# Column tiles by seven products: sums made in open PSUM banks and copied out by ScalarE, instead of added on VectorE

## The chip, the cores and the metric

The kernel runs on one core of a Trainium2 chip. A core has five engines that work side by side and wait for one another by semaphores: TensorE (PE; its weight loads are the row PEld), VectorE (DVE), ScalarE (ACT), GpSimd (POOL) and SyncE (SP), which here issues the transfers between the chip's memory and SBUF. TensorE writes its results to PSUM, which has eight banks of 128 x 512 float32; VectorE and ScalarE read them from there. The metric is the device time of one execution in microseconds (us), less being better; a run's time stands beside that of the kernel before on the same chip.

## The reference

One decoder layer over 2048 tokens (and 16 meta tokens ahead of them) of width 1024. A wide projection of the normalised input feeds two attention branches and four gates:

```python
xn = rms_norm(h, norm_gain[l])
proj = xn @ w_in[l]
sb_q, sb_k, sb_v, sw_q, sw_k, sw_v, sb_z, sw_z, g_sb, g_sw = jnp.split(proj, offsets, axis=-1)
o_sb = stick_breaking_attention(...)
...
o_sw = sliding_window_sink_attention(...)
y_sb = (o_sb * jax.nn.silu(sb_z)) @ w_branch_sb[l]
y_sw = (o_sw * jax.nn.silu(sw_z)) @ w_branch_swa[l]
merged = jax.nn.sigmoid(g_sb) * y_sb + jax.nn.sigmoid(g_sw) * y_sw
h = h + merged @ w_out[l]
```

The change touches how a part of the gates is made: `silu(sb_z)`, `silu(sw_z)`, `sigmoid(g_sb)` and `sigmoid(g_sw)`, each a block of columns of `proj` followed by its function.

## The kernel before

**Tiles and precision.** The projection is cut into column tiles of 128 columns and groups of 512 tokens (four groups, 0 to 3). The first half of the kernel treats groups 2 and 3, the second groups 0 and 1. Each factor is split into a high and a low part (`wh`, `wl` for weights, `xh`, `xl` for the input), and a product of a weight and an input takes three matmuls: high by high, high by low, low by high. A plain column tile over one group runs over 8 blocks of 128 of the width: 24 matmuls (line 1188).

**Pairs.** In a stage of each half, column tiles are made two at a time (`gate_pairs`). Two tiles c and d, two token groups `ga` and `gb` and the two halves of the width form a product of 2 x 2 blocks, which is made with seven block products instead of eight, by sums and differences of blocks. A block product is 4 blocks of the width by three matmuls, so 12 matmuls (lines 1929 to 1931). The first half has eight pairs, the second four. `t1` to `t4` are combinations of the input blocks, made once; `s1` to `s4` are combinations of the weight blocks, made for each pair by `pair_weights`: VectorE makes four sums (`r1` to `r4`), ScalarE rounds each to its high part (line 1877), VectorE subtracts to get the low part (line 1879). In the first half `pair_weights` also splits the loaded weights themselves (ScalarE line 116, VectorE line 120); in the second half the split weights come from memory. There are three buffers for `wh` and `wl` and four for the high and low parts of `s`, so those of the next pair are written as TensorE finishes with the ones in use.

**What happens behind the products, before.** Each of the seven products goes to a PSUM bank of its own, in turn over six banks (the tags g, z and t with two each). ScalarE copies the first product (line 1953), and VectorE makes seven additions of a PSUM bank and an SBUF tile (line 1935), which give the four results of a pair. A result then gets its function: ScalarE's sigmoid (lines 1940 and 1943), for the `z` gates a multiplication on VectorE (line 1941), and a store. The results, the `r` and the sigmoids all live in nine buffers of 128 x 512 named `tmp`.

**Beside the pairs.** `along` is a generator that the loop advances once per pair. In the first half it is `sums_ahead`, which loads the next half's rows and squares them on ScalarE (line 1892, four squares a step), and ends with a logarithm and an exponential (lines 133 and 134). In the second half it is `output_weight_sums`, loads, VectorE sums and stores for the last stage. `between`, at the last pair of the first half, scales the next half's input (`prep`).

**Order.** TensorE's instructions run in the order in which they are written. ScalarE's and SyncE's in these stages, and VectorE's from the middle of the first pair on, are put in order at build time by a planner, which walks through its own model of the times and takes, for an engine that is free, the earliest written instruction that can go. On the chip each engine then keeps that order strictly, whatever the times turn out to be.

Of the kernel before, what the change touches and what calls it, by code (L numbers as in the profile page):

```python
# [10 lines left out]
AF = mybir.ActivationFunctionType  # L11
# [5 lines left out]
P = 128  # L17
# [32 lines left out]
def tile_kernel(ctx, tc, x, xt, meta, metat, gain, w_in, w_sb, w_sw, w_out, sinks, fgain,  # L50
# [8 lines left out]
    def DMA(dst, src):  # L59
        return nc.sync.dma_start(*(t.bitcast(F32) if t.dtype == F32R else t for t in (dst, src)))  # L60
# [6 lines left out]
    def ps(tag):  # L67
        return pp.tile([P, 512], F32, tag=tag, name="ps_" + tag, bufs={"g": 2, "z": 2, "t": 2, "o": 2}[tag])
# [1043 lines left out]
    def tmp(dt=F32, rows=P):  # L1112
        return tp.tile([rows, GT], dt, tag="tmp", name="tmp", bufs=9)
# [112 lines left out]

    sums_back = []

    def sb_k(p):
        def use(g, acc, ms):  # L1230
            h, l = tmp(F32R), low(acc)
            evac_split(h, l, acc)
            for i, t in enumerate((h, l)):
                DMA(kd[p][g][i][:, :GT], t)
            if ms is not None:
                def later():
                    mc = meta_cols(sums_back[p] if p < 2 else ms, "t" if p < 2 else "o")
                    h, l = tmp(F32R)[:, :NM], tmp(F32R)[:, :NM]
                    A.copy(h, mc)
                    V.tensor_tensor(l, mc, f32(h), op=ALU.subtract)  # L1240
                    for i, t in enumerate((h, l)):
                        DMA(kd[p][3][i][:, GT:], t)
                pending.append(later)
        return weights(C_SBK + p * P), use, True

    def sb_q(p):
        def use(g, acc, ms):
            h, l = tmp(F32R), low(acc)
            evac_split(h, l, acc, 0.125)
            DMA(qd[p][g][0], h)  # L1250
            DMA(qd[p][g][1], l)
        return weights(C_SBQ + p * P), use, False

    def to_rows(acc, hv, lv):

# [24 lines left out]
            for queue in (soon, late, pending):  # L1280
                flush(queue)

    def sb_v(p):

        def use(g, acc, ms):
            t, d = tmp(), tmp()
            A.copy(t, acc)
            V.tensor_tensor(d[:, :GT - 1], t[:, 1:], acc[:, :GT - 1], op=ALU.subtract)
            A.copy(vf[:, p, g % 2 * 4:g % 2 * 4 + 4], t.rearrange("p (b q) -> p b q", b=4)[:, :, 0])

            def join(nxt):
                V.tensor_tensor(d[:, GT - 1:], nxt, t[:, GT - 1:], op=ALU.subtract)
                if g % 2 == 0:
                    A.copy(vn[:, p:p + 1], t[:, 0:1])

# [12 lines left out]

            def meta():
                mc = meta_cols(ms)  # L1310
                m = tmp()
                mv, md = m[:, :NM + 1], m[:, 32:32 + NM]
                G.memset(mv[:, NM:], 0.0)
                A.copy(mv[:, :NM], mc)
                V.tensor_tensor(md, mv[:, 1:], mv[:, :NM], op=ALU.subtract)
                join(mv[:, 0:1])

                def turned():
                    tr = ps("t")
                    T.transpose(tr[:NM, :P], md, ident)  # L1320
                    meta_rows(tr[:NM, :P], vm[0:NM, p, :, 0:64], vm[0:NM, p, :, 64:128])
                    for n in (NM, 2 * NM, 4 * NM):
                        DMA(vm[n:2 * n, p], vm[0:n, p])
                    rows()
                soon.append(turned)

            if ms is None:
                join(vn[:, p:p + 1] if g % 2 else vf[:, p, 4:5])
            pending.append(rows if ms is None else meta)
            if g % 2 == 0:  # L1330
                for a, t in enumerate(vfirst):
                    r = slice(64 * a, 64 * a + 64)
                    G.tensor_copy(t[r, p], vf[r, p])
        return weights(C_SBV + p * P), use, "back"

    def gate(c0, dst, silu):
        def use(g, acc, ms):
            e = tmp()
            A.activation(e, acc, AF.Sigmoid)  # L1339
            if silu:  # L1340
                V.tensor_tensor(e, acc, e, op=ALU.mult)
            DMA(dst[g], e)
        return weights(c0), use, False

    def tiles_by_tile(makes, groups, meta=False, bank="g"):
        for mk in makes:
# [570 lines left out]
    def gate_pairs(ga, gb, pairs, pool, sums_x, nxt, ordered, along, between):  # L1917

        t1, t2, t3, t4 = sums_x[:4]
        b11, b21 = ((xh[ga][:, j:j + HK, :], xl[ga][:, j:j + HK, :]) for j in (0, HK))  # L1920
        b22 = xh[gb][:, HK:, :], xl[gb][:, HK:, :]

        banks = iter(range(1 << 30))

        def product(a, b):
            acc = ps("gzt"[next(banks) % 3])
            (wh, wl), (h, l) = a, b
            for k in range(HK):
                T.matmul(acc, lhsT=wh[:, k, :], rhs=h[:, k, :], start=k == 0, stop=False)  # L1929
                T.matmul(acc, lhsT=wh[:, k, :], rhs=l[:, k, :], start=False, stop=False)  # L1930
                T.matmul(acc, lhsT=wl[:, k, :], rhs=h[:, k, :], start=False, stop=k == HK - 1)  # L1931
            return acc

        def add(t, acc, u):
            V.tensor_tensor(t, acc, u, op=ALU.add)

        def gate_out(dst, t, silu):
            if silu:
                e = tmp()
                A.activation(e, t, AF.Sigmoid)  # L1940
                V.tensor_tensor(t, t, e, op=ALU.mult)
            else:
                A.activation(t, t, AF.Sigmoid)
            DMA(dst, t)

        for n, ((_, cdst, csilu), (_, ddst, dsilu)) in enumerate(pairs):
            a11, a12, a22, s1, s2, s3, s4 = nxt
            end = n + 1 == len(pairs)
            if n and not end:
                nxt = []  # L1950
                drain(pair_weights(pairs[n + 1][0][0], pairs[n + 1][1][0], pool, nxt))
            p, u, v, w = (tmp() for _ in range(4))
            A.copy(p, product(a11, b11))
            more = product(a12, b21)
            add(u, product(s2, t2), p)
            add(p, more, p)
            if not n:
                nxt = []
                ordered()
                drain(pair_weights(pairs[1][0][0], pairs[1][1][0], pool, nxt))  # L1960
            gate_out(cdst[ga], p, csilu)
            next(along, None)
            if end:
                between()
# [5 lines left out]
            gate_out(cdst[gb], v, csilu)  # L1970
            add(u, product(s3, t3), u)
            add(w, p5, u)
            gate_out(ddst[gb], w, dsilu)
            add(u, p4, u)
            gate_out(ddst[ga], u, dsilu)


    sbt = [lambda p=p, f=f: f(p) for f, p in ((sb_k, 0), (sb_k, 1), (sb_q, 0), (sb_v, 0), (sb_v, 1), (sb_q, 1),
                                              (sb_k, 2), (sb_v, 2), (sb_q, 2), (sb_k, 3), (sb_v, 3), (sb_q, 3))]
    sbz, swz, gsb, gsw = ([(c + p * P, dst[p], dst in (zs, zw)) for p in range(len(dst))]  # L1980
                          for c, dst in ((C_SBZ, zs), (C_SWZ, zw), (C_GSB, gs), (C_GSW, gw)))
    specs = (gsb + gsw[:6] + swz + sbz + gsw[6:], sbz + gsb + gsw)

    halves = ([2, 3], [0, 1])
    g0, g1 = halves[0]
# [165 lines left out]
    held = pending[:]  # L2151
    del pending[:]
    for half, groups in enumerate(halves):
        gts = [lambda spec=spec: gate(*spec) for spec in specs[half]]
        if half == 1:
            with tc.tile_pool(name="fast1", bufs=1, side="left") as bp:
                byhand, hand = ExitStack(), ExitStack()
# [5 lines left out]
                pairs = list(zip(swz[::2], swz[1::2]))  # L2163
# [88 lines left out]
            drain(side)  # L2252
        if half == 0:
            with tc.tile_pool(name="fast", bufs=1, side="left") as bp:
                pairs = list(zip(specs[0][-FAST::2], specs[0][-FAST + 1::2]))
# [120 lines left out]
```

## Time and profile before

| | |
|---|---|
| runs, median of 3 | 2048.16 us (2047.28 to 2048.32) |
| span of the profiled execution, first to last instruction | 2045.8 us |
| TensorE busy | 2031.7 us (99%), 10375 matmuls |
| VectorE busy | 1649.3 us (81%) |
| ScalarE busy | 1177.5 us (58%) |
| the pairs' stage, first half | about 581 to 734 us |
| the pairs' stage, second half | about 778 to 854 us |

The profiled execution's time is known as its span; the runs' times include what lies around it. The profile gives, for groups of instructions, the line, engine, operation, tiles written and read and count, then busy time, the mean duration in ns, and the idle time of the engine before them with what ended it. In the order of time a row is the start, the duration, the instruction, and in brackets the idle time before it and its releaser. Busy time on TensorE overlaps: a matmul of 128 x 512 is shown with 0.39 us, but one starts every 0.23 us.

### The profile page before, as it was taken

The numbers are of one execution on the slowest core, as the hardware profiler recorded it, in microseconds if no ns is written. First come the engines' busy times: TensorE is split into PE (matmuls) and PEld (weight loads), VectorE is DVE, ScalarE is ACT, GpSimd is POOL, SyncE is SP. The second block draws the span as 40 slices with busy tenths as digits, with TensorE's granted clock in tenths as the row PEclk, the third lists the DMA queues.
The fourth block names the chain that finished last, engine by engine and source line by source line (L and its number), as shares of the span: only waits on it lengthen the run. The fifth ranks groups of instructions, "written<-read, shape, count | busy, mean of one in ns | idle before, by whom it ended". The sixth has DMA issues, their size and how long they took to land.

```text
span 2045.8 us, 31245 instructions
## 1 busy us (share of the span) xinstructions
PE 2031.7 (99%) x10375; PEld 1706.3 (83%) x10375; DVE 1649.3 (81%) x2708; ACT 1177.5 (58%) x2825; POOL 311.4 (15%) x642
## 2 busy tenths in 40 slices
PE   9999999999999999999999999999999999999998
PEld 7888888888888888888888888888888888887887
DVE  7898986877788789658887389999997788788788
ACT  6677775576755343358777366667766442335234
POOL 1233444431000000003333101000000003000000
PEclk9999999999999999999999999999999999999999
DMA  9855554865468669844344554344323779886942
GB/s 336 321 197 199 179 200 165 260 194 170 135 233 306 228 214 315 309 147 162 132 178 150 173 156 116 115 127 126 109 83 105 266 257 313 290 284 200 307 150 98
DMA packets 184065, 409.32 MB, mean 200 GB/s; under 512 B 25280, under 2 KB 29760, under 8 KB 183904
## 3 DMA queue, kind: packets, MB, share of 16 engines
q1 hardware_dynamic: 183616, 407.06, 59.0%
q8 instruction: 82, 1.34, 0.3%
q14 instruction: 79, 0.65, 0.1%
q10 hardware_dynamic: 288, 0.27, 0.0%
HBM read 256.36 MB, written 148.32 MB: 198 GB/s over the span
## 4 chain that ended last, share of the span: by engine, by line
PE 95%; ACT 2%; DVE 2%; DMA 1%; issue 1%; POOL 0%; SPq 0%; ACTq 0%; DVEq 0%; POOLq 0%
PE ps_g L1188 35%; PE ps_o L1700 6%; PE ps_z L1643 6%; PE ps_t L1668 6%; PE ps_z L1188 3%; PE ps_z L1484 3%; PE ps_o L1540 2%; PE ps_t L1518 1%; PE ps_g L1929 1%; PE ps_g L1930 1%; PE ps_g L1931 1%; PE ps_o L338 1%; PE ps_o L337 1%; PE ps_o L339 1%; PE ps_z L1929 1%; PE ps_z L1930 1%
## 5 line engine op out<-in xcount | busy, mean ns | idle before, releaser
L1188 PE MATMUL ps_g<-xh,wh 128*128 128x512 f32 x1088 | 442.3, 406 | 0.1
L1188 PE MATMUL ps_g<-xl,wh 128*128 128x512 f32 x1088 | 426.2, 392 | 0.7 <-DVE xl L2001 0.6
L1188 PE MATMUL ps_g<-xh,wl 128*128 128x512 f32 x1088 | 425.7, 391 | 0.0
L1653 DVE TENSOR_TENSOR_SCAN row<-row 128x512 f32<-128x512 f32 (+4 forms) x256 | 288.6, 1128 | 47.6 <-POOL row L1648 30.7
L1188 PEld LDWEIGHTS ps_g<-xh,wl 128*128 128x128 f32 x1088 | 204.2, 188 | 45.5 <-DVE wl L2049 0.4
L1646 ACT ACTIVATE row<-ps_z 128x512 f32<-128x512 f32 (+4 forms) x352 | 175.1, 509 | 110.3 <-PE ps_z L1643 106.3
L1188 PEld LDWEIGHTS ps_g<-xl,wh 128*128 128x128 f32 x1088 | 205.3, 189 | 34.5 <-DVE xl L2001 2.0
L1188 PEld LDWEIGHTS ps_g<-xh,wh 128*128 128x128 f32 x1088 | 204.9, 188 | 34.1 <-ACT xh L2000 0.6
L128 DVE SCALAR_TENSOR_TENSOR wtl<-ps_t,wth 128x512 fp32r<-128x512 f32 (+1 forms) x320 | 188.2, 588 | 11.3 <-ACT wth L127 11.1
L127 ACT ACTIVATE wth<-ps_t 128x512 fp32r<-128x512 f32 (+1 forms) x320 | 171.6, 536 | 41.9 <-PE ps_t L1668 39.4
L1643 PE MATMUL ps_z<-kt,q 128*128 128x512 f32 (+4 forms) x704 | 184.1, 350 | 0.7 <-ACT row L1646 0.7
L1668 PE MATMUL ps_t<-ident,row 128*128 128x128 f32 x1088 | 172.3, 273 | 1.8 <-DVE wtl L128 1.6
L1668 PEld LDWEIGHTS ps_t<-ident,row 128*128 128x128 f32 x1088 | 133.1, 140 | 35.7 <-DVE wtl L128 5.8
L1643 PEld LDWEIGHTS ps_z<-kt,q 128*128 128x128 f32 x704 | 123.8, 188 | 24.1 <-ACT row L1646 3.1
L1700 PE MATMUL ps_o<-wth,vc 128*128 128x512 f32 (+1 forms) x320 | 134.9, 422 | 0.0
L1492 ACT ACTIVATE sc<-sc,nm 128x129 f32<-128x129 f32 x256 | 100.0, 393 | 30.3 <-DVE nm L1490 29.2
L1700 PE MATMUL ps_o<-wtl,vc 128*128 128x512 f32 (+1 forms) x320 | 116.6, 364 | 0.2 <-DVE wtl L128 0.2
L1659 POOL COPY mr<-row 128x16 f32<-128x16 f32 x128 | 33.3, 263 | 382.3 <-DVE row L1653 347.7
L1477 POOL COPY sc<-skb 128x4 f32<-128x4 f32 x64 | 16.0, 256 | 458.0 <-PE ps_g L1931 304.0
L1339 ACT ACTIVATE tmp<-ps_g 128x512 f32<-128x512 f32 x63 | 37.8, 599 | 78.7 <-PE ps_g L1188 72.7
L1651 DVE TENSOR_TENSOR_SCAN row<-row,mask 128x512 f32<-128x512 f32 (+2 forms) x64 | 69.6, 1093 | 16.1 <-ACT row L1646 16.0
L1524 POOL TENSOR_SCALAR_AFFINE_SELECT pm<-ph 64x256 fp32r<-64x256 f32 x128 | 62.2, 486 | 114.7 <-ACT ph L127 110.5
(926 smaller groups left out, 4684.3 us busy)
## 6 DMA issues: line engine op xcount, KB each, us to landing
wh<-h_in_w_in SPq DMA_DIRECT2D x66, 512.0 KB, 4.0
wl<-l_in_w_in SPq DMA_DIRECT2D x66, 512.0 KB, 5.3
raw<-in_w_in SPq DMA_DIRECT2D x57, 512.0 KB, 5.6
h_in_w_in<-wh SPq DMA_DIRECT2D x50, 512.0 KB, 3.1
l_in_w_in<-wl SPq DMA_DIRECT2D x50, 512.0 KB, 4.2
q<-qd SPq DMA_DIRECT2D x128, 128.0 KB, 3.1
vc<-vd SPq DMA_DIRECT2D x48, 256.0 KB, 3.1
kd<-tmp SPq DMA_DIRECT2D x32, 256.0 KB, 3.2
```

Of the source, the lines that this page charges most:

```text
L127: A.activation(h, acc, AF.Copy, scale=scale)
L128: V.scalar_tensor_tensor(l, acc, scale, f32(h), op0=ALU.mult, op1=ALU.subtract)
L1188: T.matmul(acc, lhsT=a[:, k, :], rhs=b[:, k, :], start=k == i == 0, stop=k == KT - 1 and i == 2)
L1484: T.matmul(acc[:, a * 256:(a + 1) * 256], lhsT=lq, rhs=kk[:, 2 * kv + hl, blk * P:(blk + 2) * P], start=hl == 0, stop=hl == 1)
L1492: A.activation(sc[:, hh, :], sc[:, hh, :], AF.Exp, bias=nm[:, hh:hh + 1], accum_out=den[:, hh:hh + 1])
L1524: G.affine_select(out=pm[to, :, c], in_=full[r, :, c], pattern=[[0, 4], [sign, HB]], compare_op=ALU.is_ge, fill=0.0, base=n - 1, channel_m ...
L1643: T.matmul(z[:, :m], lhsT=qt[:, j * P:(j + 1) * P], rhs=kt[h][:, k0 + c:k0 + c + m], start=t == 0, stop=t == 1)
L1646: A.activation(r[:, c:c + m], z[:, :m], AF.Sigmoid, scale=-1.0)
L1651: V.tensor_tensor_scan(r[:, :w], r[:, :w], mask[:, :w], 1.0, op0=ALU.mult, op1=ALU.max)
L1653: V.tensor_tensor_scan(r[:, :w], r[:, :w], r[:, :w], last[j] if n else 1.0, op0=ALU.mult, op1=ALU.min)
L1668: T.transpose(tr[:, j * P:(j + 1) * P], rows_of[h, g, n - (j > i), j][:, k0:k0 + P], ident)
L1700: T.matmul(o[:, :n], lhsT=v, rhs=r, start=first and r is wh, stop=last)
```

## The change

In both stages the first pair goes on as before (`separate`). All others are made by `opened`, with three banks instead of seven. The first bank takes product 1, is copied by ScalarE, takes product 3 on top of it, is copied, takes product 5 on top, is copied, and takes product 7. The second bank takes product 2. The third takes product 4, is copied, and takes product 6 on top. So the running sums form in PSUM, and a matmul that adds to a bank has to wait for the copy out of it. VectorE adds three times per pair (one of them between two SBUF tiles), ScalarE copies four times. The products come in another order: the one with `s1` is now the fourth, `s3` the fifth, `s4` the sixth and `a22` the seventh (before: `s4`, `a22`, `s1`, `s3`). The last result's sigmoid reads the PSUM bank. The gates are put out by the same `use` function as those of plain column tiles, which for that gets the weights' loader as an argument; that part makes no instruction of its own.

```diff
-        def product(a, b):
-            acc = ps("gzt"[next(banks) % 3])
+        def product(a, b, acc=None, stop=True):
+            start = acc is None
+            if start:
+                acc = ps("gzt"[next(banks) % 3])
...
+        def copied(acc):
+            t = tmp()
+            A.copy(t, acc)
+            return t
...
+        def separate(w, cuse, duse, middle):
+            a11, a12, a22, s1, s2, s3, s4 = w
             p, u, v, w = (tmp() for _ in range(4))
             A.copy(p, product(a11, b11))
             more = product(a12, b21)
             add(u, product(s2, t2), p)
             add(p, more, p)
...
+            middle()
+            out_of(cuse, ga, p)
+            yield
             p3 = product(s4, b22)
             p4 = product(a22, t4)
             p5 = product(s1, t1)
             add(v, p5, u)
             add(v, p3, v)
...
+        def opened(w, cuse, duse):
+            a11, a12, a22, s1, s2, s3, s4 = w
+            one = product(a11, b11, stop=False)
+            p = copied(one)
+            other = product(a12, b21)
+            product(s2, t2, one, False)
+            u = copied(one)
+            add(p, other, p)
+            out_of(cuse, ga, p)
+            yield
+            two = product(s1, t1, stop=False)
+            w = copied(two)
+            product(s3, t3, one, False)
+            v = copied(one)
+            product(s4, b22, two)
+            add(w, w, v)
+            out_of(duse, gb, w)
+            add(u, two, u)
+            out_of(cuse, gb, u)
+            product(a22, t4, one)
+            duse(ga, one, None)
...
+            steps = opened(this, cuse, duse) if n else separate(this, cuse, duse, middle)
+            next(steps)
+            next(along, None)
+            if end:
+                between()
+            drain(steps)
```

More of the change, by code (lines that the diff above doesn't have):

```diff
@@ L1227, in tile_kernel, with sb_k @@
     sums_back = []
-    def sb_k(p):
+    def sb_k(p, w=weights):
         def use(g, acc, ms):
@@ L1243, in use, with sb_q @@
                 pending.append(later)
-        return weights(C_SBK + p * P), use, True
-    def sb_q(p):
+        return w(C_SBK + p * P), use, True
+    def sb_q(p, w=weights):
         def use(g, acc, ms):
@@ L1251, in use @@
             DMA(qd[p][g][1], l)
-        return weights(C_SBQ + p * P), use, False
+        return w(C_SBQ + p * P), use, False
     def to_rows(acc, hv, lv):
@@ L1281, in flush_all, with sb_v @@
                 flush(queue)
-    def sb_v(p):
+    def sb_v(p, w=weights):
         def use(g, acc, ms):
@@ L1333, in use, with gate @@
                     G.tensor_copy(t[r, p], vf[r, p])
-        return weights(C_SBV + p * P), use, "back"
-    def gate(c0, dst, silu):
+        return w(C_SBV + p * P), use, "back"
+    def gate(c0, dst, silu, w=weights):
         def use(g, acc, ms):
-            e = tmp()
+            e = acc if spare[0] and not silu else tmp()
             A.activation(e, acc, AF.Sigmoid)
@@ L1342, in use @@
             DMA(dst[g], e)
-        return weights(c0), use, False
+        return w(c0), use, False
     def tiles_by_tile(makes, groups, meta=False, bank="g"):
@@ L1923, in gate_pairs, with out_of @@
         banks = iter(range(1 << 30))
-        def product(a, b):
-            acc = ps("gzt"[next(banks) % 3])
+        def product(a, b, acc=None, stop=True):
+            start = acc is None
+            if start:
+                acc = ps("gzt"[next(banks) % 3])
             (wh, wl), (h, l) = a, b
             for k in range(HK):
-                T.matmul(acc, lhsT=wh[:, k, :], rhs=h[:, k, :], start=k == 0, stop=False)
-                T.matmul(acc, lhsT=wh[:, k, :], rhs=l[:, k, :], start=False, stop=False)
-                T.matmul(acc, lhsT=wl[:, k, :], rhs=h[:, k, :], start=False, stop=k == HK - 1)
-            return acc
+                T.matmul(acc, lhsT=wh[:, k, :], rhs=h[:, k, :], start=start and k == 0, stop=False, skip_group_check=True)
+                T.matmul(acc, lhsT=wh[:, k, :], rhs=l[:, k, :], start=False, stop=False, skip_group_check=True)
+                T.matmul(acc, lhsT=wl[:, k, :], rhs=h[:, k, :], start=False, stop=stop and k == HK - 1, skip_group_check=True)
+            return acc
+        def copied(acc):
+            t = tmp()
+            A.copy(t, acc)
+            return t
         def add(t, acc, u):
             V.tensor_tensor(t, acc, u, op=ALU.add)
[L1937 to L1951, printed above, removed]
+        def out_of(use, g, t):
+            spare[0] = True
+            use(g, t, None)
+            spare[0] = False
+        def separate(w, cuse, duse, middle):
+            a11, a12, a22, s1, s2, s3, s4 = w
             p, u, v, w = (tmp() for _ in range(4))
@@ L1956, in gate_pairs @@
             add(p, more, p)
[L1957 to L1964, printed above, removed]
+            middle()
+            out_of(cuse, ga, p)
+            yield
             p3 = product(s4, b22)
@@ L1969, in gate_pairs, with middle @@
             add(v, p3, v)
-            gate_out(cdst[gb], v, csilu)
+            out_of(cuse, gb, v)
             add(u, product(s3, t3), u)
             add(w, p5, u)
-            gate_out(ddst[gb], w, dsilu)
+            out_of(duse, gb, w)
             add(u, p4, u)
-            gate_out(ddst[ga], u, dsilu)
-    sbt = [lambda p=p, f=f: f(p) for f, p in ((sb_k, 0), (sb_k, 1), (sb_q, 0), (sb_v, 0), (sb_v, 1), (sb_q, 1),
+            out_of(duse, ga, u)
+        def opened(w, cuse, duse):
[14 more added lines that the diff above has]
+            add(w, w, v)
+            out_of(duse, gb, w)
+            add(u, two, u)
+            out_of(cuse, gb, u)
+            product(a22, t4, one)
+            duse(ga, one, None)
+        for n, ((_, cuse), (_, duse)) in enumerate(pairs):
+            end = n + 1 == len(pairs)
+            this = nxt
+            if n and not end:
+                nxt = []
+                drain(pair_weights(pairs[n + 1][0][0], pairs[n + 1][1][0], pool, nxt))
+            def middle():
+                nonlocal nxt
+                nxt = []
+                ordered()
+                drain(pair_weights(pairs[1][0][0], pairs[1][1][0], pool, nxt))
+            steps = opened(this, cuse, duse) if n else separate(this, cuse, duse, middle)
[4 more added lines that the diff above has]
+            drain(steps)
+    sbt = [lambda w=weights, p=p, f=f: f(p, w) for f, p in ((sb_k, 0), (sb_k, 1), (sb_q, 0), (sb_v, 0), (sb_v, 1), (sb_q, 1),
                                               (sb_k, 2), (sb_v, 2), (sb_q, 2), (sb_k, 3), (sb_v, 3), (sb_q, 3))]
@@ L1982, in tile_kernel, with pairs_of @@
     specs = (gsb + gsw[:6] + swz + sbz + gsw[6:], sbz + gsb + gsw)
+    def pairs_of(makes):
+        made = [mk(lambda c0: c0)[:2] for mk in makes]
+        return list(zip(made[::2], made[1::2]))
     halves = ([2, 3], [0, 1])
@@ L2153, in tile_kernel @@
     for half, groups in enumerate(halves):
-        gts = [lambda spec=spec: gate(*spec) for spec in specs[half]]
+        gts = [lambda w=weights, spec=spec: gate(*spec, w) for spec in specs[half]]
         if half == 1:
@@ L2162, in tile_kernel @@
                 *sums_x, late_lows, side = combined_anew(*groups, rs1, bp, short)
-                pairs = list(zip(swz[::2], swz[1::2]))
+                pairs = pairs_of([lambda w, spec=spec: gate(*spec, w) for spec in swz])
                 nxt = []
@@ L2254, in tile_kernel @@
             with tc.tile_pool(name="fast", bufs=1, side="left") as bp:
[L2255 removed]
+                pairs = pairs_of(gts[-FAST:])
                 sums_x = combined(*groups, bp, short, *early)
```

## The prediction

> **What bounds the kernel now.** I read the page's first part, then the waits of TensorE, then busy time by windows over the stage that changes, then that stage's groups on ScalarE and VectorE, then the order of time at the spots that decide.
>
> ```profile
> span 2045.8 us, 31245 instructions
> PE 2031.7 (99%) x10375; PEld 1706.3 (83%) x10375; DVE 1649.3 (81%) x2708; ACT 1177.5 (58%) x2825; POOL 311.4 (15%) x642
> ```
> ```profile
> PE ps_t L1668 <- DVE wtl L128: 1.6, 5, 0.5
> PE ps_o L91 <- POOL mx L88: 1.3, 1, 1.3
> PE ps_g L337 <- ACT ringl L343: 0.7, 1, 0.7
> PE ps_z L1643 <- ACT row L1646: 0.7, 2, 0.4
> PE ps_o L338 <- DVE ringl L458: 0.7, 1, 0.7
> PE ps_g L1188 <- DVE xl L2001: 0.6, 1, 0.6
> ```
> TensorE (PE) is busy in all but 2045.8 - 2031.7 = 14.1 us, and its waits for VectorE (DVE) among these rows are 1.6 + 0.7 + 0.6 = 2.9 us. None is on L1929 to L1931, the products that change. So a lighter VectorE has nothing to give back here, while each wait added to TensorE is paid in full: no later gap is wide enough to absorb it. The windows, one pair of column tiles each (us, then busy time by engine):
>
> ```profile
> 580.00:599.00 19.00, 19.00 (x85) 15.75 (x84) 17.81 (x27) 12.53 (x23) 0.00 (x0) 1.00 0.75 256
> 599.00:618.00 19.00, 18.99 (x84) 15.25 (x83) 15.48 (x25) 14.97 (x35) 0.00 (x0) 1.00 0.99 359
> 618.00:637.00 19.00, 19.00 (x85) 15.75 (x84) 15.24 (x29) 14.22 (x25) 0.00 (x0) 1.00 1.02 389
> 675.00:694.00 19.00, 19.00 (x86) 15.73 (x85) 14.29 (x23) 7.44 (x11) 0.00 (x0) 1.00 0.61 222
> ```
> The columns are PE, PEld, DVE, ACT, POOL, granted clock, DMA share and GB/s. TensorE is full and its clock 1.00. ScalarE (ACT) works 15.0 of 19 us in the second pair and 7.4 in a later one: early in the stage it also squares next half's rows. The early pairs are where a new duty of ScalarE costs most.
>
> **The change, part by part.** *Work.* A pair keeps 7 products of 12 matmuls, four gates and four stores, so TensorE, POOL and DMA bytes stay; SyncE's four stores leave in another order. Seven VectorE additions become three, one ScalarE copy becomes four, in 7 pairs of the first half and 3 of the second.
>
> ```profile
> L1935 DVE TENSOR_TENSOR tmp<-ps_g,tmp 128x512 f32<-128x512 f32 x18 | 12.3, 686 | 5.4 <-PE ps_g L1931 5.2
> L1953 ACT COPY tmp<-ps_g 128x512 f32<-128x512 f32 x3 | 1.7, 575 | 0.0
> L1877 ACT CAST sh<-tmp 128x512 fp32r<-128x512 f32 x28 | 16.9, 615 | 17.0 <-PE ps_t L1930 7.2 <-PE ps_g L1930 5.0 <-PE ps_z L1930 2.9
> L116 ACT CAST wh<-raw 128x1024 fp32r<-128x1024 f32 x15 | 15.8, 1051 | 13.6 <-PE ps_g L1930 4.6 <-DMA raw<-in_w_in 4.4 <-PE ps_t L1930 3.3
> ```
> Per pair VectorE loses 4 x 0.686 = 2.7 us (of 14.3 in the window at 675) and ScalarE gains 3 x 0.575 = 1.7 us (7.4 to 9.1). In total that is 27 us less on VectorE, worth nothing as TensorE never waits for it in the stage, and 17 us more on ScalarE, hidden in idle time if it comes at the right moment.
>
> *Moment.* This is the real edit. Before, each product had a bank of its own, and a late reader delayed nobody until that bank came round again, six products on. Now products 1, 3, 5 and 7 fill one bank and 4 and 6 another; product 3 may not begin before ScalarE has copied product 1's sum, 5 not before the copy of 3, 6 of 4, 7 of 5. Behind the waiting matmul stands the whole of TensorE's queue, and behind that the casts of the next pair's weights, whose buffers TensorE releases. Between two such products lies one product in another bank. Its length, in the second pair of the first half (the first that changes):
>
> ```profile
> 602.19 0.39 PE L1931 MATMUL ps_z<-xh,wl 128*128 128x512 f32 x1
> 602.42 0.39 PE L1929 MATMUL ps_t<-xh,wh 128*128 128x512 f32 x1
> 605.14 0.42 PE L1929 MATMUL ps_g<-t2h,sh 128*128 128x512 f32 x1
> ```
> Product 1 ends at 602.19 + 0.39 = 602.58 and product 3 begins at 605.14: 2.56 us of cover, 1.98 after a copy of 0.58. A copy that starts within 1.98 us costs nothing; beyond that, each microsecond is one of the kernel's. The old trace has copies of product 1, and shows how they stand in ScalarE's order:
>
> ```profile
> 606.34 0.62 ACT L1943 ACTIVATE tmp<-tmp 128x512 f32<-128x512 f32 x1
> 607.94 1.05 ACT L116 CAST wh<-raw 128x1024 fp32r<-128x1024 f32 x1 [0.98 <-DMA raw<-in_w_in]
> 610.37 0.62 ACT L1943 ACTIVATE tmp<-tmp 128x512 f32<-128x512 f32 x1
> 610.90 0.61 ACT L1892 ACTIVATE xs<-xs 128x512 f32<-128x512 f32 x1
> 613.62 0.19 ACT L1892 ACTIVATION_READ_ACCUMULATOR xs<-xs 128x1 f32 x1
> 613.71 1.13 ACT L1877 CAST sh<-tmp 128x512 fp32r<-128x512 f32 x2
> 614.74 0.58 ACT L1953 COPY tmp<-ps_z 128x512 f32<-128x512 f32 x1
> ```
> The copy of a sum finished at 602.58 runs at 614.74, 12.2 us late, behind gates of the first pair, casts and squares. The program up to product 3 of this pair is untouched, so what the planner had put ahead of the copy before then stays ahead. Only the two casts at 613.71 leave: the first waits for product 3, which now waits for the copy. So the copy starts when the squares end: 613.62 plus about 0.1, done at 613.7 + 0.58 = 614.3, and product 3 starts there in place of 605.14: **+9.2 us**. Bounds: had the planner taken the copy ahead of the four squares, after the gate at 610.37 (ScalarE starts its next work 0.53 later, 610.90), it ends at 611.5, +6.3; ahead of the gate at 606.34 it ends at 606.9, +1.8; at once, 0. If the two casts somehow stay, 615.32 - 605.14 = 10.2. I take 9.2, the order that the trace has.
>
> In the Trainium skill, PSUM — Partial Sum Buffer, section "Engine vs sequencer instructions", ScalarE's queue is called strict FIFO. The trace agrees: nothing passes the cast that waited 0.98 us for its load at 607.94. Without that rule the sum would lose the 9.2.
>
> After this, TensorE runs 9.2 us behind its old times while squares and loads, which don't wait for it, keep theirs; so the early pairs 3 and 4 are relieved. What may still meet a copy is the chain of the next half's row scales on ScalarE, with three table loads:
>
> ```profile
> 630.80 1.28 ACT L133 ACT_TABLE_LOAD   x1
> 635.69 0.63 ACT L1940 ACTIVATE tmp<-tmp 128x512 f32<-128x512 f32 x1
> ```
> It holds ScalarE's order for 4.9 us. A copy due at its head is late by 4.9 - 1.98 = 2.9 us, one due elsewhere by nothing. I take the middle, **+1.4 us**.
>
> *Second half.* Its first changed pair:
>
> ```profile
> 802.28 0.39 PE L1929 MATMUL ps_g<-t2h,sh 128*128 128x512 f32 x1
> ```
> ```profile
> 802.39 0.63 ACT L1940 ACTIVATE tmp<-tmp 128x512 f32<-128x512 f32 x1 [0.57 <-DVE tmp L1935]
> 806.88 0.62 ACT L1877 CAST sh<-tmp 128x512 fp32r<-128x512 f32 x1 [3.86 <-DVE tmp L1863]
> 807.40 0.58 ACT L1953 COPY tmp<-ps_z 128x512 f32<-128x512 f32 x1
> ```
> Product 3 began at 802.28. The cast at 806.88 overwrites weights that product 3 reads, so it now comes behind the copy; the copy follows the gate, 802.39 + 0.63 = 803.0, ends at 803.6: **+1.3 us**. Bounds: 0, and 807.98 - 802.28 = 5.7 if the order stays.
>
> *Other pairs and copies.* Copies of products 3, 4 and 5 have no row in this stage. The nearest is the finish, where banks are kept open in the same way: the wait of L337 for the copy L343 above, 0.7 us, once. So 0 to 0.7 per copy, 0 to 21 us for 30 copies; once in a whole stage is near 0, and I take 0. The releases of weights come in the new order of products, and each still has most of a pair (19 us) until its next use. At the pair's end the gates need fewer steps, so the nine `tmp` buffers come free earlier; VectorE's relief works the same way.
>
> Against this stands the Trainium skill, Perfetto Trace Analysis, section "Matmuls": independent groups should rotate through banks so that reading one out overlaps the next. The change keeps a product in another bank between, and by that rule the whole change would cost nothing, 2048.2. The row at 614.74 says the reader was 12.2 us late, so I don't follow it.
>
> **Sum.** 9.2 + 1.4 + 1.3 = 11.9 us on a span of 2045.8 gives 2057.7. The median of the runs shown, 2048.16, stands 2.36 us above that span; with it the forecast is **2060.1**.
>
> **The rivals.** *Hidden after all*: the planner takes each copy when it is ready, TensorE never waits, 2048.2. For it: ScalarE is 39% busy in the windows from 637 on (7.44 of 19). Against: the order above came from the same planner and the same program up to that point.
>
> *Every pair pays.* In the steady pairs the copy came late too:
>
> ```profile
> 662.60 1.06 ACT L116 CAST wh<-raw 128x1024 fp32r<-128x1024 f32 x1 [1.27 <-PE ps_t L1930]
> 663.56 0.58 ACT L1953 COPY tmp<-ps_z 128x512 f32<-128x512 f32 x1
> ```
> Product 3 began there at 662.63, and the copy ended at 664.14: if that cast, which waits for product 2, stays ahead, 1.5 us in each of the five pairs that cast such weights for a successor, 7.5 in all, 2067.6. With the 0.7 for other copies at their bound, 2088. For it: the row. Against: ScalarE idled 1.27 us there with the sum finished, so the copy lacked a `tmp` buffer rather than its turn, and buffers are freer now.
>
> *Faster*: VectorE's relief lets later stages be laid closer. Its price is at most the 2.9 us of waits for VectorE, 2045.3; it decides only with more than 4.1 us, which would have to come from a reshuffled order in stages that the change doesn't touch. That is an accident of planning; I give it 2043.
>
> **How the numbers follow.** Stall of the first pairs 0.50, hidden 0.22, every pair 0.20, faster 0.08. Within 0.2% (4.1 us, about what this measurement tells from no change) is the hidden case: faster 0.08, same 0.22, slower 0.70. The likeliest case's own range is 2054 to 2067, from 6.3 at the first pair with nothing else, to 10.2 + 2.9 + 5.7. The whole reaches from 2046.5, inside the hidden case, to 2078, half of the way from 2067.6 to 2088: that leaves out the faster case and the upper tail.
>
> **What would show it.** In the new profile, TensorE's waits should name the copy's line on ScalarE: one wait of about 9 us near 605 and one of 1 to 2 us near 812, in the order of time squares directly ahead of the first copy, and VectorE's additions down by 40. Many equal waits of about 1.5 us on the same line would mean the second rival; no such wait, the first. The prediction is wrong if the copy near 603 runs within 2 us of its product: then the planner's order was not what the old trace made me believe.

## The result: 18.3 us slower, and the profile after

| | before | after |
|---|---|---|
| median of the runs shown | 2048.24 us (2047.28 to 2049.05) | 2066.56 us (2065.58 to 2067.28) |
| ratio | | 1.0093, 95% interval 1.0078 to 1.0107 |
| time and span of the profiled execution | span 2045.8 us | 2065.58 us, span 2063.9 us |

One of the ten executions of the run `order` below had a mean granted clock of 0.56 and took 3396 us; its ratio leaves that one out.

The page of the changed kernel, first part:

```profile
span 2063.9 us, 31258 instructions
PE 2035.7 (99%) x10375; PEld 1707.7 (83%) x10375; DVE 1625.4 (79%) x2668; ACT 1192.8 (58%) x2855; POOL 312.0 (15%) x642
```

TensorE makes the same 10375 matmuls. Its idle time is 2063.9 - 2035.7 = 28.2 us where it was 14.1, and its busy time is 4.0 us longer: 14.1 + 4.0 = 18.1 us, the whole difference of the spans. VectorE has 40 instructions less (1649.3 to 1625.4 us), ScalarE 30 more (1177.5 to 1192.8). Neither is what one pays for. TensorE's waits between 575 and 870 us, where both stages of pairs lie and where before had none (us in total, times, longest):

```profile
PE ps_z L1931 <- ACT tmp L1938: 11.4, 3, 9.8
PE ps_g L1931 <- ACT tmp L1938: 0.9, 1, 0.9
PE ps_g L1931 <- ACT sh L1874: 0.5, 1, 0.5
PE ps_g L1933 <- DVE sl L1879: 0.4, 1, 0.4
```

L1938 is the copy out of an open bank. Four waits name it, 12.3 us in all, and one of them is 9.8. ScalarE and TensorE in order of time around it:

```profile
612.31 0.61 ACT L1892 ACTIVATE xs<-xs 128x512 f32<-128x512 f32 x1
...
614.35 0.63 ACT L1892 ACTIVATE xs<-xs 128x512 f32<-128x512 f32 x1
614.89 0.19 ACT L1892 ACTIVATION_READ_ACCUMULATOR xs<-xs 128x1 f32 x1
614.98 0.56 ACT L1938 COPY tmp<-ps_z 128x512 f32<-128x512 f32 x1
```
```profile
615.60 0.79 PE L1931 MATMUL ps_z<-t2h,sh 128*128 128x512 f32 x1 [9.78 <-ACT tmp L1938]
616.19 0.63 PE L1932 MATMUL ps_z<-t2l,sh 128*128 128x512 f32 x1
...
620.37 0.40 PE L1933 MATMUL ps_z<-t2h,sl 128*128 128x512 f32 x1
620.61 0.40 PE L1931 MATMUL ps_g<-xh,sh 128*128 128x512 f32 x1
```

The copy of product 1 stands behind the last four squares, and product 3 waits 9.78 us for it. The next rows show a second loss: a matmul takes 0.63 us in place of 0.39, and the next starts 0.43 us later, not 0.23. By windows (us, busy time of PE, PEld, DVE, ACT, POOL, then granted clock, DMA share, GB/s):

```profile
605.50:615.50 10.00, 0.33 (x2) 0.00 (x0) 7.92 (x12) 8.65 (x21) 0.00 (x0) 0.73 1.02 360
615.50:620.50 5.00, 4.90 (x12) 3.89 (x13) 0.69 (x1) 0.05 (x1) 0.00 (x0) 0.52 0.97 354
620.50:640.00 19.50, 19.50 (x88) 16.11 (x87) 11.43 (x23) 15.69 (x28) 0.00 (x0) 1.00 0.66 248
```

The clock granted to TensorE is 0.52 for some 5 us after the wait. Setting the matmuls of the two traces side by side by their place in TensorE's order gives the lag of each over its old time:

| where, in the changed kernel | lag gained, us |
|---|---|
| start of the kernel, loads | 0.6 |
| first half, second pair: product 3 | 9.9 |
| the eleven matmuls behind it | 2.1 |
| first half, all other pairs | 0 |
| second half, first pair (not changed): `s4` late, twice | 1.5 |
| second half, second pair: product 3, then product 6 | 0.9 + 1.2 |
| second half, fourth pair: product 3 | 1.2 |
| steps under 0.2 us in between | the rest |

### The profile page after: what moved, and what is told of

Read it like the earlier page. It is cut to its first block, busy times and chain, and to the rows that moved or that the text cites. A ratio compares the mean times of both kernels' runs of the same rounds, so it can differ in the third digit from the quotient of the medians.

```text
span 2063.9 us, 31258 instructions
## 1 busy us (share of the span) xinstructions
PE 2035.7 (99%) x10375; PEld 1707.7 (83%) x10375; DVE 1625.4 (79%) x2668; ACT 1192.8 (58%) x2855; POOL 312.0 (15%) x642
## 4 chain that ended last, share of the span: by engine, by line
PE 82%; DVE 8%; DMA 6%; ACT 3%; issue 1%; SPq 0%; POOL 0%; DVEq 0%; ACTq 0%
PE ps_g L1188 33%; PE ps_o L1700 6%; PE ps_z L1643 6%; PE ps_t L1668 6%; PE ps_z L1484 3%; PE ps_o L1540 2%; PE ps_z L1931 1%; PE ps_z L1932 1%; PE ps_z L1933 1%; PE ps_t L1518 1%; PE ps_o L338 1%; PE ps_o L337 1%; PE ps_o L339 1%; DMA ot<-xs 1%; PE ps_z L1188 1%
```

## Experiments

The theory: a copy comes late for its place in the planner's order, and TensorE, whose queue is strict and which has nothing idle to absorb it, pays every microsecond. The questions: which pairs pay, is it ScalarE's order or the `tmp` buffers behind it, what holds the second half, and are the new order of products and VectorE's relief worth anything? The comparisons of before in these runs were 2048.2 to 2048.4 us.

**One half at a time.** `half0` has open banks in the first half only, `half1` in the second only.

```diff
-            steps = opened(this, cuse, duse) if n else separate(...)
+            steps = opened(this, cuse, duse) if n and len(pairs) == 8 else separate(...)   # half0; half1: == 4
```


> Open banks in the first half only; the second half's pairs as before. Theory A: the first half's part of the loss, 12.0 us, stays: 2048.2 + 12.0 = 2060.2. If the second half's loss is only a late effect of the first half's shift, it stays too: 2066.

> Open banks in the second half only; the first half's pairs as before. The changed kernel lost 5.4 us between 768 and 858 us in small steps. Theory A (these are the second half's own, copies behind gates that VectorE delivers late): 2048.2 + 5.4 = 2053.6, or 2052 if the two steps of its first pair, which is made as before, belong to the first half's shift. Rival (they are all effects of the shift): 2048.2.

Measured: half0 2060.19 us (ratio 1.0061, 1.0046 to 1.0076), half1 2054.68 us (1.0034, 1.0021 to 1.0047). 12.0 + 6.5 = 18.5 us, against 18.3 for both: the halves pay separately. half0 is the expected 2060.2 to the tenth, but by 9.2 of wait, 1.7 of half-rate matmuls and 1.2 at the second half's first pair, where I had added 9.9 and 2.1: the tenth is luck. Half1 costs 1 us more than expected. TensorE's waits there, between 798 and 858 us:

```profile
PE ps_z L1931 <- ACT tmp L1938: 4.0, 3, 2.3
PE ps_g L1931 <- ACT tmp L1938: 0.4, 1, 0.4
```

**The first half: which pair pays.** `third` computes the second pair of the first half separately too, so that open banks begin with the third; `fourth` begins with the fourth, and leaves the second half as before.

```diff
+            steps = opened(this, cuse, duse) if n > (len(pairs) == 8) else separate(...)    # third
+            steps = opened(this, cuse, duse) if n > 2 and len(pairs) == 8 else separate(...) # fourth
```


> The changed kernel, but the second pair of the first half is made as before too; open banks begin there with the third pair (the second half is unchanged from the changed kernel). Theory A (one copy of one pair stands behind squares in ScalarE's order: 9.9 us of waiting and 2.1 us of matmuls at half rate behind it): all of that goes, 2066.6 - 12.0 = 2054.6. Rival B (whichever pair is the first with open banks pays, so the wait moves to the third pair): 2064 to 2067. Rival C (every changed pair pays about the same, one of ten is gone): 2064.7.

> The first half's second and third pairs are computed separately like its first, as is the whole second half; open banks only in the first half's fourth to eighth pairs. Theory A (a copy costs only where it stands behind the squares of the row sums on ScalarE, and these are done by the fourth pair): no wait for a copy longer than 0.5 us in the first half, and 2048 to 2050 (up to 1.4 us at the second half's first pair, where half0 also lost it). Rival B (each pair in open banks costs a little, five of seven are left): the 12.0 us of half0 shared out by pairs, so about 2048.2 + 5/7 x 12.0 = 2056.8. Rival C (open banks gain something once nothing waits): under 2046.

Measured: third 2057.16 us (1.0048, 1.0033 to 1.0063), 9.4 less than the changed kernel, not 12. TensorE's waits before 770 us, then ScalarE (the profiled execution was the longest of its four, 2061.09 us):

```profile
PE ps_t L1931 <- ACT tmp L1938: 2.6, 1, 2.6
```
```profile
626.42 0.62 ACT L1892 ACTIVATE xs<-xs 128x512 f32<-128x512 f32 x1
626.95 0.19 ACT L1892 ACTIVATION_READ_ACCUMULATOR xs<-xs 128x1 f32 x1
627.04 0.56 ACT L1938 COPY tmp<-ps_t 128x512 f32<-128x512 f32 x1
```

Now the third pair pays: 2.6 us behind a square, and 1.4 for matmuls at the lower clock. In the changed kernel, where TensorE came to this pair 12 us late, it had cost nothing. `fourth` measured 2051.52 us (1.0017, 1.0008 to 1.0026), against my 2048 to 2050 and the 2056.8 of an equal price for each pair. Its wait, and ScalarE:

```profile
PE ps_g L1931 <- ACT tmp L1938: 1.4, 1, 1.4
```
```profile
644.00 1.04 ACT L116 CAST wh<-raw 128x1024 fp32r<-128x1024 f32 x1
644.95 0.58 ACT L1938 COPY tmp<-ps_g 128x512 f32<-128x512 f32 x1
```

The squares are done, but a weight's cast stands ahead of the copy, and the four pairs behind it pay nothing. So wherever open banks begin, the first such pair waits (9.8, 2.6, 1.4 us), less the later it lies; the others of the first half don't. Why it is less is not shown.

**ScalarE's order, or the buffer behind it?** `vcopy` lets VectorE make the copies, four in each of the ten changed pairs and so 40 (its expectation says 30, which is what the change added). `own` gives the first copy of the second pair a buffer of the ring `tt`, which has three and stands nearly unused there, in place of one of the nine of `tmp`. `own3` is half0 with the first three copies of each pair in that ring.

```diff
-            t = tmp(); A.copy(t, acc)
+            t = tmp(); V.tensor_copy(t, acc)                  # vcopy, all 40 copies
+            t = short() if own else tmp(); A.copy(t, acc)      # own: p of one pair; own3: p, u, w
```


> The changed kernel, but the copy of product 1 in the second pair of the first half goes to a buffer of another ring (tt) instead of a tmp buffer. The planner then sets that copy behind the sixth square, ahead of two squares, two casts and three gates that stood ahead of it. Theory A1 (the planner had no tmp buffer for the copy, and that put it so late): the copy runs at about 605.7 to 606.3 in place of 614.98, a wait of about 1 us is left, 2066.6 - 11 = 2055.6. Rival (ScalarE has too much to do there whatever the order): the wait moves to the next copies, 2062 or more.

> The changed kernel with its 30 copies made by VectorE in place of ScalarE. Theory A (the long wait in the first half is ScalarE's order: squares ahead of the copy): the wait of 9.8 us and the half-rate matmuls behind it go, 12.0 us less in the first half; the second half, where buffers of the ring tmp and VectorE's waits for loads hold the copies, keeps its 4 to 6.5 us: 2052 to 2056. Rival B (the planner has no free tmp buffer for the copy in that pair, whichever engine makes it): the wait stays within 3 us of what it was, and 2063 to 2068. Rival C (VectorE becomes the bound where it stands waiting for loads): over 2068.

> half0 (open banks in the first half alone) with the first three of each pair's four copies written to the ring tt, three buffers that stand nearly unused in this stretch, in place of tmp. Theory A (the planner puts a copy behind the squares where its plan has no free tmp buffer): in the second pair the first copy moves ahead of six of the twelve squares, as in own, the second ahead of three and the third behind them; the waits there fall from 9.2 us to about 0.8 + 0.5 and TensorE keeps its clock, the third pair may still lose what it lost in third (2.6 us, and 1.4 at half rate), so 2050.7 to 2055. Rival B (own's result repeats: the wait only moves on to the next copy): 4 to 6 us in the second pair, 2056 to 2060. Rival C (three buffers are too few and the ring tt takes the place of tmp as the hold in all pairs): over 2060.

`vcopy` took 2080.28 us (1.0161, 1.0148 to 1.0175). I had expected 2052 to 2056. TensorE's waits before 770 us, and VectorE at the copy:

```profile
PE ps_z L1931 <- DVE tmp L1938: 13.2, 2, 10.0
```
```profile
615.14 0.69 DVE L1872 TENSOR_TENSOR tmp<-raw,tmp 128x512 f32<-128x512 f32 x1
615.74 0.69 DVE L1938 COPY tmp<-ps_z 128x512 f32<-128x512 f32 x1
```

The wait is the same 10 us on an engine that has no squares to make: the squares filled the time, they did not cause it. The rival that named the buffers was right on that wait; beyond it VectorE, which also waits for loads, is the worse place for the copies: the second half lost 17 us, where the changed kernel lost under 6. In `own` (2062.91 us; 1.0074, 1.0057 to 1.0091) the copy with a buffer of its own moves from 614.98 to 605.28:

```profile
605.28 0.56 ACT L1938 COPY tt<-ps_z 128x512 f32<-128x512 f32 x1
...
613.78 1.12 ACT L1877 CAST sh<-tmp 128x512 fp32r<-128x512 f32 x2
614.81 0.57 ACT L1938 COPY tmp<-ps_z 128x512 f32<-128x512 f32 x1
```
```profile
PE ps_z L1931 <- ACT tmp L1938: 6.0, 3, 3.8
...
PE ps_z L1931 <- ACT tt L1938: 0.7, 1, 0.7
```

Its wait falls from 9.8 to 0.7, and the next copy, still in `tmp`, is now the late one, 3.8 us, with 1.7 us of half-rate matmuls behind it. So in the profiled executions the first half loses 6.7 us in place of 12.4. The second half, whose source is the same, loses 8.7 in place of 5.2, for a reason not shown; `own` gained 3.7 us by the medians and not 11. With three copies in the ring, `own3` took 2052.32 us (1.0022, 1.0013 to 1.0032), 7.9 less than half0 and inside the expected 2050.7 to 2055:

```profile
606.00 0.56 ACT L1938 COPY tt<-ps_z 128x512 f32<-128x512 f32 x1
...
613.13 0.56 ACT L1938 COPY tt<-ps_z 128x512 f32<-128x512 f32 x1
...
615.45 0.57 ACT L1938 COPY tt<-ps_g 128x512 f32<-128x512 f32 x1
```
```profile
PE ps_z L1931 <- ACT tt L1938: 2.2, 2, 1.4
```

9.2 us of waits became 2.2, and no matmul ran slow. So the planner had placed the copies late because its plan had no `tmp` buffer free. On the chip it was otherwise: followed through the program's buffer addresses and semaphores, the buffer that the copy at 614.98 writes had been free since the last store out of it landed at 606.6. ScalarE kept the planned order all the same.

**The lower clock.** `filler` puts 42 matmuls, into a bank that nobody reads, in front of product 3 of that pair.

```diff
+                for i in range(42):
+                    T.matmul(spin, lhsT=a11[0][:, i % HK, :], rhs=b11[0][:, i % HK, :], start=True, stop=True)
             product(s2, t2, one, False)
```


> The changed kernel with 42 matmuls more between the second and the third product of the first half's second pair, into a bank that nobody reads. Theory A (the eleven matmuls at 0.427 us after the wait are due to the granted clock of 0.5 that follows TensorE's idle time): 42 x 0.227 = 9.5 us of the 9.9 us wait are filled, the copy comes at the same time, the following matmuls run at 0.227 us, and the time falls by 2.1 us to about 2064.4. Rival B (the slow matmuls come from something else in that stretch, such as the transfers beside them at a DMA share of 0.99 or the weight loads): they stay at 0.427 us and the time is within 0.7 us of 2066.6. Rival C (the fillers come later than the copy would, or displace it): over 2067.5.

```profile
605.59 9.68 PE L1979 MATMUL ps_o<-xh,wh 128*128 128x512 f32 x42
615.11 0.39 PE L1931 MATMUL ps_z<-t2h,sh 128*128 128x512 f32 x1
615.33 0.39 PE L1932 MATMUL ps_z<-t2l,sh 128*128 128x512 f32 x1
```

2062.75 us (1.0076, 1.0062 to 1.0090), 3.8 us less for 42 matmuls more. In the windows from 605 to 625 the granted clock is 1.00, and product 3 runs at 0.23 us a matmul. Against the changed kernel product 3 begins 0.5 us earlier, as the planner also drew the copy forward, and product 4 2.8 us earlier; the rest came in small steps, up and down. So the eleven slow matmuls were the clock's, at a DMA share of 1.04 too. The Trainium skill, TensorE: Matmul & The Clock Gate, section "What's actually happening", tells of a half-rate state after an idle window of some 3.4 us, and its section "Wait — 56ns, not 53.3ns?" of 426.7 ns between cold matmuls of this size; the 0.427 us between the slow matmuls here agree.

**The second half.** In half1 VectorE and ScalarE (bracket: idle time before, and its releaser):

```profile
820.54 0.69 DVE L1908 TENSOR_TENSOR xs<-xs 128x512 f32<-128x512 f32 x1 [4.57 <-DMA xs<-in_w_out]
...
822.95 0.68 DVE L1942 TENSOR_TENSOR tmp<-ps_g,tmp 128x512 f32<-128x512 f32 x1
...
824.75 0.68 DVE L1341 TENSOR_TENSOR tmp<-tmp 128x512 f32<-128x512 f32 x1
```
```profile
825.53 0.59 ACT L1938 COPY tmp<-ps_z 128x512 f32<-128x512 f32 x1 [0.68 <-DVE tmp L1341]
...
834.38 0.58 ACT L1938 COPY tmp<-ps_g 128x512 f32<-128x512 f32 x1 [2.05 <-DMA zw<-tmp]
```

VectorE waits 4.57 us for a load of the output weights' sums. Behind it stand the pair's addition and gate; the gate holds a `tmp` buffer, and the copy at 825.53 waits for it, the one at 834.38 for a store to give its buffer back. So here the shortage is real. `nosub` leaves out the 32 subtractions of these sums in half1; loads and stores stay, and what is stored is the loaded weight. `fixed` leaves nothing out: copies as in own3, open banks in both halves, and the 32 subtractions on GpSimd.

```diff
-            V.tensor_tensor(b11, b12, b11, op=ALU.subtract)    # and three more: nosub
+            G.tensor_tensor(b11, b12, b11, op=ALU.subtract)    # and three more: fixed
```


> half1 with the 32 subtractions of the output weights' sums left out in the second half (their loads and stores stay; what is stored is the loaded weight, so the output is another). Theory A (VectorE stands at the first subtraction waiting for its load, the additions and gates behind it keep tmp buffers, and the copies wait for those): the waits of the first product group on a copy go from 4.4 us to under 1, and 2048 to 2050. Rival B (the DMA engines, busy 0.9 and more there, land the stores of the gates late, and these hold the buffers): traffic is the same, 2053 to 2055.

> The changed kernel with the copies in the ring tt in the first half as in own3, and the 32 subtractions of the output weights' sums made by GpSimd in place of VectorE in the second half; nothing is left out. Theory A (VectorE's turn at those subtractions is what holds the second half's copies): the second half adds less than 1 us to own3's time, where half1 added 6.5. Rival B (the second half's cost is the transfers', as its DMA engines are busy): it adds 4 to 6.5 us to own3's time. Under 2046 neither expects: TensorE has nothing to gain.

`nosub` took 2049.27 us (1.0007, 0.9998 to 1.0016), with no wait of TensorE for a copy, and copies are now made as soon as their product ends:

```profile
819.34 0.59 ACT L1934 COPY tmp<-ps_z 128x512 f32<-128x512 f32 x1 [2.06 <-PE ps_z L1929]
```

The same transfers, no loss: VectorE's turn at the subtractions held the buffers. `fixed`, at 2055.99 us (1.0043, 1.0028 to 1.0058), bears it out in part: GpSimd now stands waiting for those loads, and of four waits for a copy in the second half one is left, the first:

```profile
POOL xs L1908 <- DMA xs<-in_w_out: 23.3, 3, 9.7
```
```profile
808.72 0.50 PE L1931 MATMUL ps_z<-t2h,sh 128*128 128x512 f32 x1 [1.79 <-ACT tmp L1938]
...
809.71 0.63 PE L1931 MATMUL ps_z<-t2h,sh 128*128 128x512 f32 x1
```
```profile
809.00:813.00 4.00, 4.00 (x12) 3.09 (x12) 2.68 (x5) 0.00 (x0) 3.90 (x2) 0.57 0.89 268
```

But that wait came with the lower clock (0.57), 1.7 us more. It is 3.7 us above own3, between the two theories (under 1, and 4 to 6.5).

**The order of products, and VectorE's relief.** `order` has no open banks, only the changed kernel's order of the last four products, in all pairs but each half's first. `fewer` is the kernel before with four of seven additions left out in the same pairs.

```diff
+                p5 = product(s1, t1); ...; product(s3, t3); ...; p3 = product(s4, b22); ...; product(a22, t4)  # order
-            add(p, more, p)     # and add(v, p3, v), add(u, s3's product, u), add(u, p4, u): fewer
```


> No open banks: all pairs separate, each product in its bank of its own and seven additions a pair, but in all pairs other than each half's first the last four products come in the changed kernel's order (s1, s3, s4, a22). Theory A (the order of the products is harmless, the copies that a later product waits for are what costs): 2048 to 2050, and no wait for a copy. Rival B (the order brings the stores of the gates later and with them the loads behind them on SP's queue, as in the second half): 2051 to 2055, with VectorE waiting over 8 us for the output weights' loads.

> The kernel before with four of the seven VectorE additions of a pair left out in all pairs but each half's first (40 additions of 0.68 us, so the output is another); banks, copies and the order of the products stay. Theory A (VectorE's additions lie beside TensorE's products, so what the change saves there buys nothing): within 1 us of the kernel before. Rival B (VectorE's relief shortens something): under 2046.

`order` 2051.00 us (1.0014, 1.0004 to 1.0023), `fewer` 2049.65 us (1.0011, 1.0002 to 1.0021). Neither waits for a copy and neither is faster. Both lose the same 1.2 us and 0.7 us in the second half's first, unchanged pair. TensorE's waits there, of `order`:

```profile
PE ps_g L1931 <- ACT sh L1874: 0.8, 1, 0.8
PE ps_g L1933 <- DVE sl L1879: 0.4, 1, 0.4
```

The two rows stand, with the lines of each kernel, in every kernel whose first half differs from before (in `filler` the second row alone), and are missing in half1 and nosub, whose first half is the same. So it is a price for changing the first half, not for open banks. I lay it to the loads of the next half's input, which leave SyncE's queue in another order and for which VectorE waits longer in all three (7.0 us at L1155 in the changed kernel, 3.4 in `order`, 4.7 in `fewer`, 2.0 before); this was not tried by itself. The expectation for `order` was 1 us too low for it.

## Why the prediction was right, and where it was not

The time, 2066.6 us, lies 6.5 us above the forecast of 2060.1 and inside the range. It lies inside the likeliest case's own range too, but only by that range's upper end, which stands for other terms than those that came: the clock is not among them, and the table loads are. That agreement is luck.

*Right: the place and the size of the first wait.* The step from the copy's row behind the squares gave 9.2 us; it measured 9.8 by the wait and 9.9 by the lag. The squares ended 1.3 us later than in the old trace. The choice among the bounds (0, 1.8, 6.3, 9.2, 10.2) was made by the order that the old trace showed, and that order held.

*Right in effect, wrong in its reason: ScalarE's order.* I put the lateness down to what stood ahead on ScalarE. `vcopy` shows 10.0 us with nothing of that ahead, and `own` and `own3` show that another buffer moves the copy. The planned lack of a `tmp` buffer placed the copy; the queue only kept it. I had that cause in hand for the steady pairs ("lacked a buffer rather than its turn") and did not carry it to the pair that mattered.

*Missed: the clock.* The sum had no term for it. 2.1 us, shown by `filler`.

*Wrong: the table loads.* Taken at 1.4 us between 0 and 2.9; measured 0, the lower bound. In the changed kernel they run from 629.4 to 633.7 us, between the copies at 626.6 and 635.7, and TensorE waits for neither.

*Under-sized: the second half.* 1.3 us for one copy. That copy cost 0.9 by the lag in the changed kernel, 1.5 in half1 and 2.1 in `fixed`, so its step was right. What failed is "other pairs and copies: 0, the `tmp` buffers come free earlier": the copies take buffers, VectorE's gates release them late behind the output weights' loads, and two more copies cost 1.2 us each. And 1.5 us came from a pair that does not change. In spans, forecast 2057.7 and measured 2063.9: +0.7 at the first wait, +2.1 clock, -1.4 table loads, +3.5 second half (1.5 + 0.9 + 1.2 + 1.2 - 1.3) and +0.6 at the start leave 0.7 in small steps.

*The rivals.* "Hidden" is false, at 9.9 us. "Every pair pays" is nearest in time, 2067.6 (its upper sum, 2067.6 + 21, is 2088.6 and not 2088), but not how it went: seven of the ten changed pairs pay nothing over 0.2 us. Its mechanism does exist, once: in `fourth` the cast stands ahead of the copy and costs 1.4 us, against my 1.5. "Faster" is refuted by `fewer`: 40 additions less bought nothing. No version with open banks beat the kernel before; `own3` at 1.0022 came nearest of those that leave nothing out and open the first half from its second pair on.

## What to carry to other kernels

A bank that is filled again right after being copied turns the copy into a part of TensorE's chain; count for each copy the cover (here 2.0 us), and look in the old trace where that copy stands, not how busy its engine is. Where a planner lays the order, ask which buffer the instruction needs: a plan that is short of buffers puts it late for good, even if the chip would have had the buffer in time, and one spare ring can be worth more (7.9 us) than a freer engine (0). Price a wait of TensorE at more than its length, for the matmuls behind it may run at half rate: here they did where 1.8 us of idle time or more fell into one period of the clock, as follows.

## What the runs showed of the hardware

A wait of TensorE of under 3 us was sometimes followed by half-rate matmuls and sometimes not: they came after 1.79 us in `fixed` (0.63 us for a matmul, granted clock 0.57) and after 2.56 us in `third`. After a wait of 2.34 us they came in `third`, but not in half1:

```profile
821.51 0.63 PE L1931 MATMUL ps_g<-xh,sh 128*128 128x512 f32 x1 [2.34 <-ACT tmp L1938]
```
```profile
826.16 0.50 PE L1931 MATMUL ps_z<-t2h,sh 128*128 128x512 f32 x1 [2.34 <-ACT tmp L1938]
```

So the length of the wait alone doesn't decide it. The granted clock answers what does. In all fourteen traces it changes only on a grid of 3.41 us that runs through the whole execution, and between the kernel's start and its end the lower stretches last 3.41, 6.83 or 10.24 us, one to three periods. The periods around the two waits, of `third` and then of half1 (behind the period and its length stands TensorE's busy time, and third from the end the granted clock):

```profile
818.32:821.73 3.41, 1.07 (x5) 0.60 (x4) 0.23 (x1) 0.86 (x2) 0.00 (x0) 1.00 1.04 411
821.73:825.15 3.42, 3.42 (x9) 2.67 (x9) 2.87 (x5) 1.25 (x3) 0.00 (x0) 0.50 1.04 394
```
```profile
821.41:824.82 3.41, 2.42 (x11) 1.68 (x9) 3.41 (x7) 1.73 (x3) 0.00 (x0) 1.00 0.57 211
824.82:828.23 3.41, 2.06 (x9) 1.73 (x10) 3.41 (x7) 0.61 (x2) 0.00 (x0) 1.00 0.94 262
828.23:831.65 3.42, 3.42 (x17) 2.84 (x16) 2.02 (x4) 1.74 (x3) 0.00 (x0) 1.00 0.99 311
```

In `third` the whole wait lies in one period, 3.41 - 1.07 = 2.34 us, and the next period runs at 0.50. In half1 the end of a period parts the wait, 1.0 and 1.3 us, and the clock stays at 1.00. The other periods of the fourteen traces agree: between start and end, each of the ten at full clock with 1.79 us (`fixed`) or more of idle time was followed by one at 0.50, and none with 1.73 us (`own`) or less was. So in these traces the limit lies between the two, near half of a period, and where the grid falls decides whether a wait in between costs more than itself. By the section of the Trainium skill named above (TensorE: Matmul & The Clock Gate, "What's actually happening") an idle window of 3.4 us comes first; none fits into the waits of 1.79 and 2.56 us, and the measurement decides.
